# Moving a store to another queue, sums of x to another engine, and read-backs over three chunks

## The chip, the cores and the metric

One core of one Trainium2 chip. The metric is device time in microseconds (us) of the whole kernel, the median of a few runs. The engines named below are TensorE (PE in the profile, PEld its weight loads), VectorE (DVE), ScalarE (ACT), GpSimd (POOL) and SyncE (SP, which here only issues DMAs). Each of ScalarE, GpSimd and SyncE can issue a DMA from its own instruction stream; instructions of one engine run in the order of the program.

## The reference

```python
def hybrid_layer(x, w_in, b_f, lam_p, subln_g, w_out, ln_g, ln_b, layer_idx):   # x (1, 512, 2048) float32
    h = x @ w_in
    (fq, fk, fv, fg, sq, sk, sv, sg, dq, dk, dv, dg, ff) = jnp.split(h, _split_points(), axis=-1)
...
    o_fox = forgetting_attention(...)              # 6 heads of 128
    o_fox = o_fox.reshape(b, s, FOX_W) * jax.nn.silu(fg)
...
    o_sb = stick_breaking_attention(...)           # 6 heads of 128
    o_sb = o_sb.reshape(b, s, SB_W) * jax.nn.silu(sg)
...
    o_d = differential_attention(...)              # 4 heads of 128, then RMS norm of each head
    o_d = of.astype(x.dtype).reshape(b, s, DIFF_W) * jax.nn.silu(dg)

    y = jnp.concatenate([o_fox, o_sb, o_d], axis=-1) @ w_out
    return _layernorm(DEEPNORM_ALPHA * x + y, ln_g, ln_b)
```

All of it is float32. One input projection makes queries, keys, values and gates of 16 heads and the forget gates; three kinds of causal attention follow, each head's output is multiplied by its gate, and one output projection, the residual and a layer norm end it.

## The kernel before

Every float32 operand of a product is split into a rounded part ("h", made by ScalarE as a cast or copy) and the rest ("l", made by VectorE as operand minus rounded part, line 121, 191 or 699), and a product is three matmuls: h times h, h times l, l times h (`mm3`). So each chunk of weights that arrives in a tile `raw` costs one cast on ScalarE and one subtraction on VectorE, and TensorE waits for the "l" part last.

**Stages.** The first stage multiplies x by the weights of the first pair's queries and keys ("f" chunks 0 to 7, 128x2x512 each, accumulators p0a to p0d): every chunk goes through the four accumulators in 36 matmuls. Then come 30 units u = 2 to 31 of four chunks each; a unit is one kind (query, key, value, gate) of one pair of heads, and it uses seven products in the place of eight (a Strassen-like scheme), so that x is needed in sums as well. The last stage is the output projection (accumulators po0a to po3d), which needs the gated outputs of all 16 heads as "m0" to "m15", each split in h and l.

**Sums of x.** x comes in eight tiles `xr` (n = 0 to 7). `split_x` makes the h and l parts used by the first stage; `x_sums` then overwrites the tile with four sums of quarter tiles (lines 331 to 334, 128x256 elements each) and splits the result into `xs_0`, `xs_1` (128x1024 each). The sums are used from unit 2 on. `x_sums(n)` is called at ticks 4n+5 of a counter that advances with the matmuls.

**Finished heads.** `gate(h)` multiplies a head's output `mx` by its gate on GpSimd (line 493) and stores it to a DRAM tensor `mixd` (line 494); the last two heads stay on chip. In the last unit, u = 31, `load_mix` reads the 14 stored heads back on ScalarE's queue (line 505) into tiles `mr` and splits them. Their places become free as x's tiles of that unit are used up, seven to a chunk.

**Order.** The program text is laid out by ticks, and a scheduler that plays a timeline then fixes the order of each engine; matmuls and a few others are pinned in the written order. SyncE fetches the weight chunks (lines 163 and 166) into three `raw` tiles, and GpSimd adds a second part onto each unit chunk by an accumulating DMA (line 172), both far ahead of use.

Of the kernel before, what the change touches and what calls it, by code (L numbers as in the profile page):

```python
# [12 lines left out]
ALU = mybir.AluOpType  # L13
# [6 lines left out]
NK = D // P  # L20
# [58 lines left out]
def trunk(ctx, tc, x, xt, w_first, w_in, w_ff, b_f, lam_p, subln_g, w_out, ln_g, ln_b, out):  # L79
    nc = tc.nc  # L80
    V, A, G, T = nc.vector, nc.scalar, nc.gpsimd, nc.tensor
# [29 lines left out]
    def mm3(ps, ah, al, bh, bl, first, last, part=None):  # L111

        if part in (None, 0):
            mm(ps, ah, bh, first, False)
        if part in (None, 1):
            mm(ps, ah, bl, False, False)
        if part in (None, 2):
            mm(ps, al, bh, False, last)
# [4 lines left out]
    def split(hi, lo, src, scale=None):  # L123

        if scale is None:
            A.copy(hi, src)  # L126
            low(lo, src, hi)
        else:
            A.activation(hi, src, AF.Copy, scale=scale)
            V.scalar_tensor_tensor(out=lo, in0=src, scalar=scale, in1=hi.bitcast(F32),  # L130
                                   op0=ALU.mult, op1=ALU.subtract)
# [7 lines left out]
    NU = 4 * len(PAIRS)  # L139
# [81 lines left out]
    def tick():  # L221
        if clock[0] in events:
            with tc.high_priority(EARLY if clock[0] > T0 else 0):
                for fn in events.pop(clock[0]):
                    fn()
        clock[0] += 1

    def load_ahead(n):
        fetch(n + AHEAD + 2)
        add_in(n + AHEAD + 1)  # L230
        if n + AHEAD < len(chunks) and n + AHEAD not in ready:
            load_chunk(n + AHEAD)
# [28 lines left out]
    def kx_pair(tags, shape, name):  # L261
        return tuple(kx.tile(shape, F32R, tag=t, name=f"{name}{s}") for t, s in zip(tags, "hl"))
# [27 lines left out]
    mixd = dram.tile([NK, P, S], F32, name="mixd")  # L290
# [3 lines left out]
    with ExitStack() as actx:  # L294
# [31 lines left out]
        def x_sums(n):  # L326


            j, i = divmod(n, 2)
            r = xraw.pop(n).rearrange("p k (b t) -> p (k b) t", b=2)  # L330
            G.tensor_tensor(out=r[:, 3], in0=r[:, 1], in1=r[:, 3], op=ALU.subtract)
            G.tensor_tensor(out=r[:, 1], in0=r[:, 1], in1=r[:, 0], op=ALU.subtract)
            G.tensor_tensor(out=r[:, 0], in0=r[:, 3], in1=r[:, 0], op=ALU.subtract)
            G.tensor_tensor(out=r[:, 2], in0=r[:, 2], in1=r[:, 0], op=ALU.add)
            xs[j][i] = kx_pair(xs[j][i], [P, 4, H2], f"xs{j}_{i}")
            split(*xs[j][i], r)

# [136 lines left out]
        def silu(h, c):  # L474

            e = wk(f"ge{h}")
            A.activation(e, c, AF.Abs)
            A.activation(e, e, AF.Exp, scale=-1.0)
            A.activation(e, e, AF.Ln, bias=1.0)
            V.scalar_tensor_tensor(out=e, in0=c, scalar=0.0, in1=e, op0=ALU.min, op1=ALU.subtract)  # L480
            A.activation(e, e, AF.Exp)  # L481
            G.tensor_tensor(out=c, in0=c, in1=e, op=ALU.mult)  # L482
            gt[h] = c
            if h in mixed:
                gate(h)
# [3 lines left out]
        def gate(h):  # L489
            mx = mixed[h]  # L490
            kt = ORDER.index(h)
            if kt < NK - 2:
                G.tensor_tensor(out=mx, in0=mx, in1=gt[h], op=ALU.mult)
                nc.sync.dma_start(mixd[kt], mx)
            else:
                V.tensor_mul(mx, mx, gt[h])
                into_slot(kt, mx)

        def into_slot(kt, src):
            mh[kt], ml[kt] = next_slot(f"m{kt}")  # L500
            split(mh[kt], ml[kt], src)

        def load_mix(kt):
            mr = wk(f"mr{kt}")
            nc.scalar.dma_start(mr, mixd[kt])
            into_slot(kt, mr)
# [119 lines left out]
        def head_out(h, aux):  # L626
            o = o_of[h]
            mx = at.tile([P, S], F32, tag="mx", name=f"mx{h}")
            A.copy(mx, o)
            if not NF + NS <= h:  # L630
                mixed[h] = mx
                if h in gt:
                    gate(h)
                return
            sq = wk(f"sq{h}")
            A.activation(sq, o, AF.Square)
            sqh, sql = wk(f"sqh{h}", F32R), wk(f"sql{h}", F32R)
            split(sqh, sql, sq)
            aux.update(mx=mx, sq=(sqh, sql))

        def sub_norm(h, aux):

            ss = psO(f"ss{h}")
            mm(ss, onesr, aux["sq"][0], True, False)
            mm(ss, onesr, aux["sq"][1], False, True)
            v = wk(f"v{h}")
            V.tensor_scalar(out=v, in0=ss, scalar1=1.0 / HD, scalar2=SUB_EPS, op0=ALU.mult, op1=ALU.add)
            y, t = wk(f"ry{h}"), wk(f"rt{h}")
            rsqrt(v, y, t)
            mx = aux["mx"]  # L650
            V.scalar_tensor_tensor(out=mx, in0=mx, scalar=g8, in1=y, op0=ALU.mult, op1=ALU.mult)
            mixed[h] = mx
            if h in gt:
                gate(h)
# [56 lines left out]
        for n in range(NJ):  # L711
            at_unit(4 * n + 5 - n // 7, lambda n=n: x_sums(n))
# [6 lines left out]
        def bank(u, b):  # L719
            return ps_p.tile([P, 512], F32, tag=f"pj{b}", name=f"p{u}{b}")  # L720
# [77 lines left out]
        for u in range(2, NU):  # L798
            pb = {}
            for j in range(NK // 4):  # L800
                load_ahead(n)
                wp = ready[n]
                xp = {5: 3, 7: 1, 6: 0, 3: 2}
                for m, pr in enumerate(SUMS_LAST if 0 < j < NK // 4 - 1 else BANKWISE):
                    if m % 2 == 0:
                        tick()
                    b, half = BANK[pr]
                    if b not in pb:
                        pb[b] = bank(u, b)
                    dst = pb[b][:, half * H2:(half + 1) * H2]  # L810
                    for i in range(2):
                        if pr == 1:
                            bh, bl = xa[j][0][:, i], xa[j][1][:, i]
                        elif pr in xp:
                            bh, bl = (s[:, xp[pr]] for s in xs[j][i])
                        else:
                            kt, cs = 4 * j + 2 + i, slice(0, H2) if pr == 2 else slice(H2, S)
                            bh, bl = xh[kt][:, cs], xl[kt][:, cs]
                        mm3(dst, wp[pr][0][:, i], wp[pr][1][:, i], bh, bl,
                            j == 0 and i == 0 and half == 0,  # L820
                            j == NK // 4 - 1 and i == 1 and (half == 1 or pr == 3))
                    if j == NK // 4 - 1:
                        with tc.high_priority(EARLY):
                            combine(u, pr, pb)
                del ready[n]
                n += 1
                if u == NU - 1 and j < 2:
                    for kt in range(7 * j, 7 * j + 7):
                        load_mix(kt)

        def out_product(n, k, kt, t, c0, ps):
# [167 lines left out]
```

## Time and profile before

| | |
|---|---|
| median of 3 runs | 1022.93 us (1016.45 to 1025.36) |
| the profiled execution | 1020.78 us, of it 1019.0 us from the first to the last instruction |
| TensorE, VectorE, ScalarE, GpSimd busy | 94%, 74%, 52%, 27% of the span |
| granted TensorE clock, mean | 0.981 |
| DRAM read and written | 151.18 MB and 12.07 MB |

The profile is of one execution. Busy shares are averages over very different stages; a stage is judged by its own window. A time in brackets behind a row of the timeline is how long the engine stood idle before it, and the arrow names what ended that.

### The profile page before, as it was taken

The numbers are of one execution on the slowest core, as the hardware profiler recorded it, in microseconds if no ns is written. First come the engines' busy times: TensorE is split into PE (matmuls) and PEld (weight loads), VectorE is DVE, ScalarE is ACT, GpSimd is POOL, SyncE is SP. The second block draws the span as 40 slices with busy tenths as digits, with TensorE's granted clock in tenths as the row PEclk, the third lists the DMA queues.
The fourth block names the chain that finished last, engine by engine and source line by source line (L and its number), as shares of the span: only waits on it lengthen the run. The fifth ranks groups of instructions, "written<-read, shape, count | busy, mean of one in ns | idle before, by whom it ended". The sixth has DMA issues, their size and how long they took to land.

```text
span 1019.0 us, 18043 instructions
## 1 busy us (share of the span) xinstructions
PE 954.7 (94%) x6944; PEld 899.6 (88%) x6944; DVE 753.0 (74%) x1284; ACT 526.9 (52%) x893; POOL 272.6 (27%) x322
## 2 busy tenths in 40 slices
PE   8798999989998998989999999999999789999994
PEld 7688989989998998979998999999999778888883
DVE  8957787779777976997899778877877853433558
ACT  6445564466455644764576556646754762221222
POOL 6822242224232321231222133223322010000026
PEclk9899999999999999999999999999999999999997
DMA  7365567656665666557656766677677732832313
GB/s 278 110 149 145 136 163 191 166 145 163 176 169 145 157 173 181 130 138 176 176 145 141 191 169 173 168 198 194 168 178 196 231 106 82 349 104 87 108 59 140
DMA packets 53406, 164.42 MB, mean 161 GB/s; under 512 B 6466, under 2 KB 7106, under 8 KB 53064
## 3 DMA queue, kind: packets, MB, share of 16 engines
q1 hardware_dynamic: 29256, 111.36, 33.3%
q0 software_dynamic: 20320, 41.43, 23.6%
q10 hardware_dynamic: 3744, 10.49, 2.8%
q8 instruction: 54, 0.88, 0.4%
q14 instruction: 32, 0.26, 0.1%
HBM read 151.18 MB, written 12.07 MB: 160 GB/s over the span
## 4 chain that ended last, share of the span: by engine, by line
PE 57%; DVE 16%; DMA 14%; issue 6%; ACT 4%; POOL 2%; ACTq 0%; POOLq 0%; DVEq 0%; SPq 0%
PE o L106 9%; DMA raw<-in_w_in_dram 9%; DVE wlt L121 4%; DMA mr<-mixd 2%; PE l L106 2%; DVE wlb L121 2%; ACT wht L126 2%; DMA kc<-qkd 1%; DMA qc<-qkd 1%; PE po0b L106 1%; PE p0a L106 1%; PE po0c L106 1%; PE po0d L106 1%; PE po2d L106 1%; PE po2c L106 1%
## 5 line engine op out<-in xcount | busy, mean ns | idle before, releaser
L172 POOL DMA_DIRECT2D raw<-in_w_in_dram x120 | 104.8, 874 | 447.1 <-DMA raw<-in_w_in_dram 221.9
L121 DVE TENSOR_TENSOR wlt<-raw,wht 128x1024 fp32r<-128x1024 f32 x120 | 151.0, 1263 | 50.5 <-ACT wht L126 49.8
L126 ACT CAST wht<-raw 128x1024 fp32r<-128x1024 f32 x120 | 124.8, 1046 | 104.2 <-DVE raw L204 70.8
L121 DVE TENSOR_TENSOR wlb<-raw,whb 128x768 fp32r<-128x768 f32 x120 | 119.7, 1002 | 25.5 <-ACT whb L126 24.9
L126 ACT CAST whb<-raw 128x768 fp32r<-128x768 f32 x120 | 99.8, 832 | 57.6 <-PE p2d L106 7.8
L203 DVE TENSOR_TENSOR raw<-raw 128x256 f32<-128x256 f32 x120 | 53.5, 448 | 28.3 <-DMA raw<-in_w_in_dram 27.3
L121 DVE TENSOR_TENSOR wl<-raw,wh 128x1024 fp32r<-128x1024 f32 x23 | 30.2, 1314 | 51.4 <-ACT wh L126 51.4
L126 ACT CAST wh<-raw 128x1024 fp32r<-128x1024 f32 x23 | 24.1, 1050 | 63.1 <-PE po2d L106 27.6
L204 DVE TENSOR_TENSOR raw<-raw 128x256 f32<-128x256 f32 x120 | 54.5, 459 | 2.2
L535 ACT ACTIVATE u<-u,m 128x128 f32<-128x128 f32 (+3 forms) x56 | 31.4, 561 | 47.1 <-DVE m L532 46.9
L907 POOL TENSOR_TENSOR y<-y,gb 128x512 f32<-128x512 f32 (+1 forms) x8 | 12.0, 1517 | 155.5 <-ACT y L906 155.5
L126 ACT CAST pth<-pt 128x128 fp32r<-128x128 f32 (+1 forms) x64 | 26.9, 421 | 14.5 <-PE pt L109 14.0
L121 DVE TENSOR_TENSOR ptl<-pt,pth 128x128 fp32r<-128x128 f32 (+1 forms) x64 | 30.9, 483 | 3.5 <-ACT pth L126 3.3
L191 DVE TENSOR_TENSOR wl<-raw,wh 128x512 fp32r<-128x512 f32 x22 | 17.1, 793 | 20.8 <-ACT wh L190 20.8
L571 DVE TENSOR_TENSOR_SCAN rs<-e 128x128 f32<-128x128 f32 (+3 forms) x24 | 19.8, 823 | 15.1 <-POOL e L568 15.1
L482 POOL TENSOR_TENSOR g<-g,ge 128x512 f32<-128x512 f32 x16 | 24.7, 1542 | 16.9 <-ACT ge L481 16.9
L190 ACT CAST wh<-raw 128x512 fp32r<-128x512 f32 x22 | 13.5, 620 | 28.6 <-PE o L106 11.1
L106 PE MATMUL o<-ptl,vh 128*128 128x256 f32 x96 | 27.6, 287 | 0.0
L106 PE MATMUL o<-pth,vl 128*128 128x256 f32 x96 | 27.4, 285 | 0.0
L548 POOL TENSOR_SCALAR_AFFINE_SELECT d<-d 128x128 f32<-128x128 f32 x24 | 16.3, 679 | 39.3 <-ACT d L547 39.3
L106 PE MATMUL o<-pth,vh 128*128 128x256 f32 x96 | 25.6, 267 | 0.0
L576 ACT ACTIVATE rs<-rs 128x128 f32<-128x128 f32 (+3 forms) x24 | 11.3, 470 | 26.8 <-POOL rs L574 26.8
(6285 smaller groups left out, 4010.6 us busy)
## 6 DMA issues: line engine op xcount, KB each, us to landing
raw<-in_w_in_dram SPq DMA_DIRECT2D x120, 640.0 KB, 4.9
raw<-in_w_in_dram POOLq DMA_DIRECT2D x120, 256.0 KB, 4.3
raw<-in_w_out_dram SPq DMA_DIRECT2D x32, 512.0 KB, 3.9
xr<-in_x_t_dram SPq DMA_DIRECT2D x7, 512.0 KB, 7.6
raw<-in_w_first_dram SPq DMA_DIRECT2D x7, 512.0 KB, 5.2
mixd<-mx SPq DMA_DIRECT2D x14, 256.0 KB, 4.1
qkd<-c POOLq DMA_DIRECT2D x14, 256.0 KB, 4.3
mr<-mixd ACTq DMA_DIRECT2D x14, 256.0 KB, 3.6
```

The source lines that it names most:

```text
L106: pin(T.matmul(ps, lhs, rhs, start=start, stop=stop))
L121: V.tensor_tensor(out=lo, in0=src, in1=hi.bitcast(F32), op=ALU.subtract)
L126: A.copy(hi, src)
L172: nc.gpsimd.dma_start(raws[n][:, 0:2], w_in[g - 2, j, :, 1:3], accum_op=ALU.add)
L190: pin(A.copy(hi, raw[:, k]))
L191: pin(V.tensor_tensor(out=lo, in0=raw[:, k], in1=hi.bitcast(F32), op=ALU.subtract))
L203: V.tensor_tensor(out=raw[:, 2], in0=raw[:, 2], in1=raw[:, 0], op=ALU.add)
L204: V.tensor_tensor(out=raw[:, 3], in0=raw[:, 3], in1=raw[:, 2], op=ALU.add)
L482: G.tensor_tensor(out=c, in0=c, in1=e, op=ALU.mult)
L535: A.activation(u[:, :n], u[:, :n], AF.Exp, bias=m, scale=-1.0, accum_out=sm)
L548: G.affine_select(out=dt_[:, i * P:n], in_=dt_[:, i * P:n], pattern=[[-1, P]], base=0, channel_multiplier=1, compare_op=ALU.is_ge, fill=BIG)
L571: V.tensor_tensor_scan(out=rv[:, :n][:, ::-1], data0=ev[:, ::-1], data1=ev[:, ::-1], initial=0.0, op0=ALU.add, op1=ALU.max)
```

## The change

Three edits. The four sums of `x_sums` are issued on VectorE in the place of GpSimd. The store of a gated head is issued on GpSimd's queue in the place of SyncE's. The 14 read-backs are issued as 4, 5 and 5 in the first three chunks of unit 31, in the place of 7 and 7 in the first two.

```diff
             r = xraw.pop(n).rearrange("p k (b t) -> p (k b) t", b=2)
-            G.tensor_tensor(out=r[:, 3], in0=r[:, 1], in1=r[:, 3], op=ALU.subtract)
-            G.tensor_tensor(out=r[:, 1], in0=r[:, 1], in1=r[:, 0], op=ALU.subtract)
-            G.tensor_tensor(out=r[:, 0], in0=r[:, 3], in1=r[:, 0], op=ALU.subtract)
-            G.tensor_tensor(out=r[:, 2], in0=r[:, 2], in1=r[:, 0], op=ALU.add)
+            V.tensor_tensor(out=r[:, 3], in0=r[:, 1], in1=r[:, 3], op=ALU.subtract)
+            V.tensor_tensor(out=r[:, 1], in0=r[:, 1], in1=r[:, 0], op=ALU.subtract)
+            V.tensor_tensor(out=r[:, 0], in0=r[:, 3], in1=r[:, 0], op=ALU.subtract)
+            V.tensor_tensor(out=r[:, 2], in0=r[:, 2], in1=r[:, 0], op=ALU.add)
...
                 G.tensor_tensor(out=mx, in0=mx, in1=gt[h], op=ALU.mult)
-                nc.sync.dma_start(mixd[kt], mx)
+                nc.gpsimd.dma_start(mixd[kt], mx)
...
-                if u == NU - 1 and j < 2:
-                    for kt in range(7 * j, 7 * j + 7):
+                if u == NU - 1 and j < 3:
+                    for kt in range(*((0, 4), (4, 9), (9, NK - 2))[j]):
                         load_mix(kt)
```

TensorE's order is the same to the last matmul. VectorE's list grows by 32 instructions and GpSimd's loses them and gains 14 DMA issues. The scheduler also moves some rows nearby.

The first place is VectorE's list in the first stage, around the "l" part of chunk 3's weights (wl_239, made from raw_174). xr_128, xr_154, xr_168, xr_172, xr_222 and xr_226 are the tiles of x for n = 0 to 5. Before, on VectorE:

```order
L121 TENSOR_TENSOR xb2l<-xr_226,xb2h 128x256
L121 TENSOR_TENSOR x11l<-xr_226,x11h 128x512
L121 TENSOR_TENSOR xs_0l<-xr_168,xs_0h 128x1024
L121 TENSOR_TENSOR wl_239<-raw_174,wh_238 128x1024
L121 TENSOR_TENSOR wl_295<-raw_180,wh_294 128x1024
L121 TENSOR_TENSOR xs_1l<-xr_172,xs_1h 128x1024
```

And now, on the same engine at the same place:

```order
L121 TENSOR_TENSOR xb2l<-xr_226,xb2h 128x256
L121 TENSOR_TENSOR x11l<-xr_226,x11h 128x512
L331 TENSOR_TENSOR xr_172<-xr_172 128x256
L121 TENSOR_TENSOR xs_1l<-xr_154,xs_1h 128x1024
L333 TENSOR_TENSOR xr_168<-xr_168 128x256
L121 TENSOR_TENSOR wl_239<-raw_174,wh_238 128x1024
L331 TENSOR_TENSOR xr_222<-xr_222 128x256
L121 TENSOR_TENSOR wl_295<-raw_180,wh_294 128x1024
```

The sums stand between the other rows, the split of xs_0 from n = 2 has gone behind wl_239, and that of xs_1 from n = 1 has come down to stand just ahead of it.

The second place is GpSimd's list at the first gated head (mx_1459). e_1 and rs_1 are tiles of an attention head's scores, raw_1434 is a weight chunk. Before, on GpSimd (the store stood on SyncE, between two weight fetches):

```order
L482 TENSOR_TENSOR g_1320<-g_1320,ge_1394 128x512
L493 TENSOR_TENSOR mx_1459<-mx_1459,g_1320 128x512
L568 AFFINE_SELECT e_1_1479<-e_1_1479 128x128
L172 DMA raw_1434<-in_w_in_dram 128x512
L574 AFFINE_SELECT rs_1_1485<-rs_1_1485 128x128
```

And now:

```order
L482 TENSOR_TENSOR g_1320<-g_1320,ge_1394 128x512
L493 TENSOR_TENSOR mx_1459<-mx_1459,g_1320 128x512
L568 AFFINE_SELECT e_1_1479<-e_1_1479 128x128
L494 DMA mixd<-mx_1459 128x512
L172 DMA raw_1434<-in_w_in_dram 128x512
L574 AFFINE_SELECT rs_1_1485<-rs_1_1485 128x128
```

The store follows its own product on the engine that made it, and the accumulating fetch comes behind it.

The third place is ScalarE's list at the end of unit 31. wh_1 is the rounded half of the output projection's first chunk, without which TensorE can't go on in po0a; wh_10147 and wh_10232 belong to the two chunks after it, m10h and m12h are read-backs. Before, on ScalarE:

```order
L126 CAST pth_2_10018<-pt_3_10151 128x4x128
L535 ACTIVATE u_0_10119,s_0_10122<-u_0_10119,m_0_10120 128x128
L765 COPY e_10170<-p31a 128x2x256
L553 ACTIVATE u_0_10119<-u_0_10119,r_0_10124 128x128
L126 CAST wh_10232<-raw_10074 128x1024
L535 ACTIVATE u_1_10211,s_1_10214<-u_1_10211,m_1_10212 128x256
L190 CAST wh_1_10080<-raw_9822 128x512
```

And now:

```order
L505 DMA mr_10141<-mixd 128x512
L126 CAST m10h<-mr_10125 128x512
L126 CAST wh_10147<-raw_9919 128x1024
L126 CAST m10h<-mr_10131 128x512
L126 CAST pth_2_10004<-pt_3_10151 128x4x128
L547 ACTIVATE d_1_10202<-cb_10082,ncq 128x256
L553 ACTIVATE u_0_10093<-u_0_10093,r_0_10098 128x128
L126 CAST m12h<-mr_10135 128x512
L765 COPY e_10170<-p31a 128x2x256
L126 CAST m12h<-mr_10141 128x512
L126 CAST wh_10232<-raw_10048 128x1024
L190 CAST wh_1_10054<-raw_9822 128x512
```

Casts of read-backs, which had all been done before this piece, now stand in it, ahead of wh_1.

## Rows read from the trace of the kernel before

**Rows 1.** The page: busy time by engine, and the chain that ended last.

```profile
PE 954.7 (94%) x6944; PEld 899.6 (88%) x6944; DVE 753.0 (74%) x1284; ACT 526.9 (52%) x893; POOL 272.6 (27%) x322
...
PE 57%; DVE 16%; DMA 14%; issue 6%; ACT 4%; POOL 2%; ACTq 0%; POOLq 0%; DVEq 0%; SPq 0%
```

**Rows 2.** Windows of the first stage: busy time of each engine, clock, DMA.

```profile
8.20:31.30 23.10, 15.72 (x92) 13.11 (x90) 23.10 (x24) 16.48 (x30) 20.25 (x19) 0.93 0.61 221
31.30:52.00 20.70, 20.66 (x122) 18.80 (x123) 20.65 (x17) 6.94 (x7) 17.23 (x15) 0.91 0.46 130
```

**Rows 3.** Timeline of TensorE: start, length, instruction, and idle time before it.

```profile
31.34 0.58 PE L106 MATMUL p0a<-xa1h,wl 128*128 128x256 f32 x1 [6.87 <-DVE wl L121]
```

**Rows 4.** The chain that ended last, first stage: start, length, what.

```profile
12.38 1.44 PE p0a L106 x7
...
18.04 1.73 PE p0a L106 x9
...
38.63 1.41 PE p0a L106 x9
...
59.73 1.41 PE p0d L106 x9
```

**Rows 5.** Timeline of VectorE in the first stage.

```profile
6.33 0.42 DVE L121 TENSOR_TENSOR xb0l<-xr,xb0h 128x256 fp32r<-128x256 f32 x1
6.66 0.42 DVE L698 CAST wh<-raw 128x512 fp32r<-128x512 f32 x1
7.00 0.68 DVE L121 TENSOR_TENSOR x2l<-xr,x2h 128x512 fp32r<-128x512 f32 x1
7.60 0.68 DVE L699 TENSOR_TENSOR wl<-raw,wh 128x512 fp32r<-128x512 f32 x1
...
13.13 0.96 DVE L121 TENSOR_TENSOR xb1l<-xr,xb1h 128x256 fp32r<-128x256 f32 x1
14.01 1.23 DVE L121 TENSOR_TENSOR x6l<-xr,x6h 128x512 fp32r<-128x512 f32 x1
...
29.54 3.41 DVE L121 TENSOR_TENSOR wl<-raw,wh 128x1024 fp32r<-128x1024 f32 x2
...
57.09 0.76 DVE L204 TENSOR_TENSOR raw<-raw 128x256 f32<-128x256 f32 x2
58.76 1.23 DVE L121 TENSOR_TENSOR wlt<-raw,wht 128x1024 fp32r<-128x1024 f32 x1 [0.92 <-ACT wht L126]
59.91 0.69 DVE L130 SCALAR_TENSOR_TENSOR ql<-qr,qh 128x512 fp32r<-128x512 f32 x1
```

**Rows 6.** Timeline around the first store, SyncE and VectorE.

```profile
134.18 0.33 SPq L494 DMA_DIRECT2D mixd<-mx  x1
...
135.69 1.22 DVE L121 TENSOR_TENSOR wlt<-raw,wht 128x1024 fp32r<-128x1024 f32 x1
...
136.93 0.33 SPq L163 DMA_DIRECT2D raw<-in_w_in_dram  x1
```

**Rows 7.** Line 454, GpSimd's own stores: ns of one, min/median/max.

```profile
L454 POOL DMA_DIRECT2D qkd<-c x14: 576/606/902, 146.7 to 768.7; - x14
```

**Rows 8.** Timeline of TensorE, unit 31 and the start of the output projection.

```profile
804.20 0.38 PE L106 MATMUL p31a<-xs_0h,wht 128*128 128x256 f32 x1 [2.75 <-ACT wht L126]
...
806.19 0.44 PE L106 MATMUL p31a<-xs_0h,wlt 128*128 128x256 f32 x1 [1.49 <-DVE wlt L121]
...
811.96 0.66 PE L109 MATMUL pt<-ident,u 128*128 128x128 f32 x4 [1.03 <-ACT u L553]
...
820.77 0.50 PE L106 MATMUL po0a<-wh,m1h 128*128 128x512 f32 x1 [1.23 <-ACT wh L190]
...
822.72 0.50 PE L106 MATMUL po0a<-wl,m1h 128*128 128x512 f32 x1 [1.45 <-DVE wl L191]
```

**Rows 9.** Timeline of ScalarE there, and the page's row of the read-backs (KB, us to landing).

```profile
810.66 0.62 ACT L126 CAST m10h<-mr 128x512 fp32r<-128x512 f32 x1 [2.53 <-DMA mr<-mixd]
...
820.12 0.60 ACT L190 CAST wh<-raw 128x512 fp32r<-128x512 f32 x1
...
mr<-mixd ACTq DMA_DIRECT2D x14, 256.0 KB, 3.6
```

## The prediction

> **What bounds the kernel now.** The busy table comes first: TensorE is busy for 94% of the span, and it holds 57% of the chain that ended last [rows 1]. So a gain can only come from a place where TensorE waits, and each of the three edits has to be tied to such a place. The windows of the first stage show one: from 8.2 to 31.3 us VectorE is busy all the time, 23.1 of 23.1 us, GpSimd 20.25 of them with the sums of x, and TensorE only 15.72; in the next 20.7 us VectorE still has no gap, and the granted clock is 0.91 of full [rows 2]. The timeline gives the wait its name: at 31.34 TensorE takes up chunk 3 after 6.87 us, released by VectorE's subtraction for that chunk's "l" part [rows 3]. The chain shows what it cost after that: in chunk 1 the third matmul starts at 12.38 and the next chunk's row at 18.04, 5.66 us; in chunk 3 it is 31.34 to 38.63, 7.29 us, 1.63 more, because the clock had fallen to its lower level (1.2 GHz) in the pause [rows 4]. Chunks 4 to 7 then run without a wait and the stage ends at 59.73 + 1.41 = 61.14 [rows 4]. The stage thus loses 6.87 + 1.63 = 8.5 us at one place, and VectorE is late there. The other place is the end of unit 31: waits of 2.75, 1.49, 1.03, 1.23 and 1.45 us within 19 us, released by ScalarE and VectorE, which have the read-backs in their lists [rows 8].
>
> **Sums of x on VectorE.** VectorE is saturated there, and it gets 32 more instructions. What decides is that its own instructions were slow while GpSimd summed. Without GpSimd, starts follow each other by 0.34 us for 128x256 (6.33, 6.66, 7.00) and 0.60 for 128x512 (7.00, 7.60), and 1.15 for 128x1024 (58.76, 59.91); beside GpSimd's sums the same 128x256 takes 0.88 (13.13, 14.01), a 128x512 lasts 1.23 instead of 0.68, and two 128x1024 last 3.41 together, about 1.7 each [rows 5]. The DMA engines are no likely cause: their share falls from 0.61 to 0.46 between the two windows of rows 2, and GpSimd's load stays.
>
> The sum up to chunk 3's "l" part goes by the orders. Before, 22 instructions stand from 8.20 to its end at about 31.25: 10 of 128x256, 7 of 128x512, 5 of 128x1024. By the fast prices they are 10 x 0.34 + 7 x 0.60 + 5 x 1.15 = 13.35 us, so some 9.7 of the 23 us are interference. Now 33 instructions stand there: one 128x1024 (the split of xs_0 from n = 2) has gone behind, and 12 sums have come ahead. That is 13.35 - 1.15 + 12 x 0.34 = 16.3, and the part is ready at 24.5 instead of 31.25. TensorE would ask for it at about 23.6 (chunks 1 and 2 gain about 0.8 from the same source), so a wait of 1 us is left and VectorE is still last, and I take it that the clock, which fell after 6.87 us, stays up after so short a pause. Gain: 31.3 - 24.5 = 6.8 of start and 1.6 of clock, **8.4 us**.
>
> Is something late next? Up to the first "l" part of stage two (from 58.76 to 59.99 before [rows 5], for TensorE's 61.14) VectorE's list now has 32 sums, 14 lows of 128x256, 11 of 128x512, 14 of 128x1024 and some 5 us of smaller work: 10.9 + 4.8 + 6.6 + 16.1 + 4.8 = 43.2 us from 8.20, so 51.4. TensorE wants it at 61.14 - 8.4 = 52.7. It fits with 1.3 us to spare; before, the margin was 1.15. The price of a sum isn't in the trace; its bounds are 0.34 and 0.88 by the rows, and I take 0.34, since L204, a sum of the same shape and in place, made two in 0.76 us at 57.09 with GpSimd idle [rows 5].
>
> The Trainium skill, SBUF — State Buffer, section on who interferes with whom, has a rule that bears on this: a VectorE instruction with two SBUF inputs and a GpSimd instruction that reads SBUF share one port as an exclusive lock, and the second to issue waits for the whole of the first. The rows agree that two-input instructions stretch, but by 0.54 us at 128x256, less than a whole sum of GpSimd; by either reading the sums alone on VectorE meet no lock, and the term stays.
>
> **Stores on GpSimd's queue.** On SyncE the store waits for GpSimd's product with the next weight fetch behind it. At the first store the fetch goes out at 136.93, 2.4 us after the store's issue ended, and just when VectorE's subtraction, which frees the `raw` tile, ends at 135.69 + 1.22 = 136.91 [rows 6]. I read the 13 other stores in the same way, and at each the next fetch leaves at the end of such a subtraction. So SyncE's relief is worth **nothing**. On GpSimd a store costs its issue, 0.58 to 0.90 us by its own stores of the same size, median 0.61 [rows 7]: 14 x 0.61 = 8.5 us of an engine that is busy for 27% [rows 1]. Queued behind it are the accumulating fetches and the masks of scores; GpSimd mostly waits for a landing or for VectorE ahead of these, which covers the issue. Ends: 0 and 14 x 0.90 = 12.6 us; I take 0. SyncE loses 14 issues, and no queue is passed by anything else.
>
> **Read-backs as 4, 5, 5.** Nothing is taken away; ten of the 28 splits come later. What gains is chunk 2's "t" part on ScalarE and VectorE: with two fewer read-backs ahead of it, 1 to 2 us of the 2.75 + 1.49 [rows 8]. What loses is wh_1: before, it stood at 820.12 with all read-backs done [rows 9]; now the casts of the last five stand ahead of it, and they are issued only at about 810 and need 3.6 us to land, during which ScalarE stands still as it did for 2.53 us at 810.66 [rows 9]. From there: landing at 814, then five casts of 0.52, two of weights of 1.0, the other softmax rows and the copy of p31a of about 2.4, and wh_1 at 820 to 821 again. So TensorE comes earlier to po0a and waits longer in it. Bounds: all waits of rows 8 gone, 8 us, and one more landing exposed, -3.6; I take **0.5 us** of gain, as the same casts are on ScalarE either way.
>
> **Sum.** 8.4 + 0 + 0.5 = 9 us. Against the profiled execution, 1020.8 - 9 = 1011.8; the median of the runs lies 2.1 higher, so 1022.9 - 9 = **1014 us**. The reordering near it, in the units of the second and third pair, moves rows by one or two places where TensorE doesn't wait; I give it 0 with 1.5 us each way.
>
> **Rivals.** Times are on the scale of the median.
>
> 1. The read-back really opens the end: half of the waits in rows 8 go, 4 us in the place of 0.5, 1010. For it: chunk 2 is freed of two splits. Against: wh_1 is now last in ScalarE's list. 17%.
> 2. The read-back closes it: one more landing of 3.6 is exposed ahead of wh_1, 1014 + 4 = 1018. For it: ScalarE's new order. 16%.
> 3. The first stage's gain is only half carried on: a late x tile or a late first chunk of stage two takes its place; 1014 + 4.3 = 1018. For it: the margin of 1.3 us. Against: every fetch that feeds it is triggered by VectorE's own earlier subtractions. 9%.
> 4. The stores hold GpSimd on the path: up to 12.6 us, 1014 + 12.6 = 1027, at half exposure 1020. For it: DMA is 14% of the chain [rows 1], and the accumulating fetches are issued behind the stores. Against: GpSimd's idle time. 6%. Here the skill speaks against the change: the same page says that a DMA issued from GpSimd can starve under VectorE's work and took 3.1 us in the place of 0.62, and by that figure 14 stores would be an estimated 43 us of GpSimd. The stores of rows 7 ran beside a VectorE that is 74% busy, and none took over 0.90.
> 5. Slower than before: the stretch was not GpSimd's doing, and VectorE gets 32 sums on top. The first "l" part of stage two then comes at 60 + 32 x 0.34 = 71 or, at the slow price, 60 + 28 = 88 instead of 61: 1033 to 1050. It decides from the point where a sum costs more than about 0.6 us with its neighbours unchanged. Against it are the fast and slow rows of the same shape. 4%.
>
> **How the numbers follow.** The forecast itself has 48%, as 1009 to 1018. The range 1007 to 1021 takes in rivals 1 to 3 and half of 4. About 1% is what a measurement of this kernel can tell from no change, that is 1012.7 and below for faster: rival 1 and a third of the forecast, with a little for noise, 0.36; slower is rival 5 and a part of 4, 0.07; the rest, 0.57, is within.
>
> **What would show it.** In the profile after: two-input instructions of VectorE at 0.34, 0.60 and 1.15 us steps from 8 to 50 us; the wait of 6.87 gone to about 1 and the clock at full there; the first stage ending near 52.7; no PE wait behind a store on GpSimd; the waits at the start of po0a longer than before and those of chunk 2 shorter. I am wrong if VectorE's steps stay at 0.88, if the stage ends early but unit 2 starts late, or if the end moves by more than 4 us.

## The result, and the profile after

The changed kernel takes 1008.43 us in the median (four runs, 1007.21 to 1010.7) against 1022.62 for the kernel before: ratio 0.9872, 95% interval 0.9824 to 0.9920, so 8 to 18 us faster. The measured median lies inside the range given (1007 to 1021), 5.6 us under the forecast of 1014 and 0.6 under the stretch of 1009 to 1018 that the forecast itself was given; it is nearest to rival 1. The profiled execution took 1007.21 us, span 1005.5, 13.5 less than before.

The start of a unit's first matmul is the best ruler through the span, since TensorE's order is the same in both:

```
start of        before    after   difference
p2 (stage two)   60.98    52.36     -8.62
p7              189.00   180.84     -8.16
p14             365.79   363.46     -2.33
p24             626.15   615.13    -11.02
p31             785.81   774.46    -11.35
po2             916.59   902.10    -14.49
```

So the first stage brings 8.6 us, the 29 units after it 2.7 net (they lose 6 and win 9), unit 31 with the start of the output projection 3.1, and 1.0 is lost behind po2, which makes 13.5.

The page's busy table, to compare with [rows 1] (the chain of the profile after goes back only to 789 us, so its shares can't be compared):

```profile
PE 954.1 (95%) x6944; PEld 903.0 (90%) x6944; DVE 744.4 (74%) x1316; ACT 528.7 (53%) x893; POOL 246.1 (24%) x304
```

VectorE has 32 instructions more and 8.6 us less busy time: what it lost was stretch. The windows of the first stage, as [rows 2] (length, then busy time of PE, PEld, DVE, ACT and POOL, clock, DMA share, GB/s):

```profile
8.20:24.50 16.30, 15.50 (x97) 13.77 (x96) 16.30 (x34) 13.04 (x25) 0.00 (x0) 1.00 0.77 284
8.20:31.30 23.10, 22.30 (x140) 19.91 (x139) 23.10 (x49) 16.82 (x30) 0.00 (x0) 1.00 0.80 292
31.30:52.00 20.70, 20.70 (x135) 18.84 (x134) 19.02 (x34) 11.00 (x14) 3.32 (x4) 1.00 0.49 111
```

VectorE does 49 instructions in the 23.1 us in which it did 24, and the granted clock is 1.00. VectorE's timeline, as [rows 5], and TensorE's wait, as [rows 3]:

```profile
12.51 0.42 DVE L121 TENSOR_TENSOR xa1l<-xr,xa1h 128x256 fp32r<-128x256 f32 x1
12.84 0.42 DVE L121 TENSOR_TENSOR xb1l<-xr,xb1h 128x256 fp32r<-128x256 f32 x1
13.18 0.69 DVE L121 TENSOR_TENSOR x6l<-xr,x6h 128x512 fp32r<-128x512 f32 x1
13.78 0.42 DVE L333 TENSOR_TENSOR xr<-xr 128x256 f32<-128x256 f32 x1
...
23.09 1.22 DVE L121 TENSOR_TENSOR wl<-raw,wh 128x1024 fp32r<-128x1024 f32 x1
...
51.31 1.23 DVE L121 TENSOR_TENSOR wlt<-raw,wht 128x1024 fp32r<-128x1024 f32 x1 [0.66 <-ACT wht L126]
...
24.36 0.38 PE L106 MATMUL p0a<-xa1h,wl 128*128 128x256 f32 x1 [0.80 <-DVE wl L121]
```

Steps are 0.34 us at 128x256 where they were 0.88, and 0.60 at 128x512. Chunk 3's "l" part ends at 24.31 (forecast 24.5), TensorE waits 0.80 us for it instead of 6.87, and VectorE comes to stage two's first "t" part at 51.31 after a gap of 0.66, so its list is no longer what is late. The part ends at 52.54; TensorE, which starts the stage at 52.36, takes it up at 53.30 and doesn't wait.

The stores: GpSimd's timeline at the first one, and line 494's own view (ns of one, min/median/max). The store's issue took 0.61 us, landings take 2.3 to 3.9 us:

```profile
125.13 0.47 POOL L568 TENSOR_SCALAR_AFFINE_SELECT e<-e 128x128 f32<-128x128 f32 x1
125.56 0.61 POOL L494 DMA_DIRECT2D mixd<-mx  x1
127.04 0.86 POOL L172 DMA_DIRECT2D raw<-in_w_in_dram  x1 [0.87 <-DMA raw<-in_w_in_dram]
...
L494 POOL DMA_DIRECT2D mixd<-mx x14: 597/613/613, 125.6 to 753.4; - x14
...
DMA to landing us min/median/max: 2.3/2.9/3.9
```

Behind the store GpSimd stood idle for 0.87 us until a landing, so the store was covered. TensorE's waits in unit 31 and at the output projection, as [rows 8], and ScalarE there, as [rows 9]:

```profile
790.86 0.39 PE L106 MATMUL p31a<-xs_0h,wht 128*128 128x256 f32 x1 [1.25 <-ACT wht L126]
793.09 0.58 PE L106 MATMUL p31a<-xs_0h,wlt 128*128 128x256 f32 x1 [1.72 <-DVE wlt L121]
806.37 0.50 PE L106 MATMUL po0a<-wh,m1h 128*128 128x512 f32 x1 [0.85 <-ACT wh L190]
808.31 0.50 PE L106 MATMUL po0a<-wl,m1h 128*128 128x512 f32 x1 [1.44 <-DVE wl L191]
...
789.76 1.05 ACT L126 CAST wht<-raw 128x1024 fp32r<-128x1024 f32 x1
...
798.46 0.62 ACT L126 CAST m9h<-mr 128x512 fp32r<-128x512 f32 x1 [0.26 <-DMA mr<-mixd]
...
804.23 0.62 ACT L126 CAST m12h<-mr 128x512 fp32r<-128x512 f32 x1 [0.84 <-DMA mr<-mixd]
804.75 1.04 ACT L126 CAST wh<-raw 128x1024 fp32r<-128x1024 f32 x1
805.70 0.61 ACT L190 CAST wh<-raw 128x512 fp32r<-128x512 f32 x1
```

The waits add up to 5.26 us instead of 7.95 (2.75 + 1.49 + 1.03 + 1.23 + 1.45), and the one for the softmax row is gone in this execution. ScalarE's last stop for a landing is 0.84 us instead of the 2.53 at 810.66. wh_1 stands at 805.70, 31.2 us after the start of unit 31; before it was 820.12 - 785.81 = 34.3.

The middle was not in the forecast. VectorE, GpSimd and TensorE at the change from unit 8 to unit 9 (c is the combination of unit 8; TensorE needs its bank b for p9b):

```profile
231.65 1.23 DVE L121 TENSOR_TENSOR wlt<-raw,wht 128x1024 fp32r<-128x1024 f32 x1 [0.38 <-ACT wht L126]
232.79 0.95 DVE L571 TENSOR_TENSOR_SCAN rs<-e 128x384 f32<-128x384 f32 x1
233.66 1.46 DVE L766 TENSOR_TENSOR e<-e 128x256 f32<-128x256 f32 x1
...
236.43 0.95 DVE L121 TENSOR_TENSOR wlb<-raw,whb 128x768 fp32r<-128x768 f32 x1
237.30 0.41 DVE L778 TENSOR_TENSOR c<-p8b,e 128x256 f32<-128x256 f32 x1
...
232.99 1.84 POOL L482 TENSOR_TENSOR g<-g,ge 128x512 f32<-128x512 f32 x1
...
237.86 0.36 PE L106 MATMUL p9b<-xs_0h,wht 128*128 128x256 f32 x1 [2.56 <-DVE c L778]
```

And before:

```profile
239.12 1.16 DVE L766 TENSOR_TENSOR e<-e 128x256 f32<-128x256 f32 x1
...
241.13 1.21 DVE L121 TENSOR_TENSOR wlt<-raw,wht 128x1024 fp32r<-128x1024 f32 x1
242.51 0.96 DVE L571 TENSOR_TENSOR_SCAN rs<-e 128x384 f32<-128x384 f32 x1 [0.17 <-POOL e L568]
243.38 0.40 DVE L778 TENSOR_TENSOR c<-p8b,e 128x256 f32<-128x256 f32 x1
...
243.93 0.36 PE L106 MATMUL p9b<-xs_0h,wht 128*128 128x256 f32 x1
```

The weight row wlt and the score row rs, which stood behind the combination's first step (L766), now stand ahead of it, and wlb and another score row (L573) have come in ahead of its step for bank b (L778). So L766 starts 0.66 us after TensorE has begun p9a (233.66 and 233.00) where it started 2.08 ahead (239.12 and 241.20). A gate product of GpSimd stretches it to 1.46 us, but it took 1.16 before as well. Unit 13 has the same wait, 2.55 us. Before, neither p9b nor p13b waited for the combination.

The waits are the smaller part of what the middle loses. These are the windows from p7 to p14, before and after (columns as above):

```profile
189.00:365.79 176.79, 165.86 (x1347) 161.86 (x1346) 144.63 (x227) 101.21 (x167) 54.47 (x72) 1.00 0.65 163
180.84:363.46 182.62, 169.78 (x1347) 167.54 (x1346) 146.04 (x227) 102.18 (x167) 59.04 (x75) 0.96 0.64 159
```

Of the 5.8 us lost, TensorE's idle time makes 1.9 (10.93 to 12.84), and the same 1347 matmuls took 3.9 us longer at a lower granted clock: it is 0.50, the level of 1.2 GHz, behind both waits, from 239.4 to 242.7 and from 341.8 to 345.1. From p14 to p24 the gain of 8.7 is 5.3 us less idle time (15.20 to 9.88) and 3.4 us of faster matmuls, at 0.99 instead of 0.97.

### The profile page after: what moved, and what is told of

It is laid out like the page before. It is cut to its first block, busy times and chain, and to the rows that moved or that the text cites. A ratio compares the mean times of both kernels' runs of the same rounds, so it can differ in the third digit from the quotient of the medians.

```text
span 1005.5 us, 18030 instructions
## 1 busy us (share of the span) xinstructions
PE 954.1 (95%) x6944; PEld 903.0 (90%) x6944; DVE 744.4 (74%) x1316; ACT 528.7 (53%) x893; POOL 246.1 (24%) x304
## 5 line engine op out<-in xcount | busy, mean ns | idle before, releaser
L121 DVE TENSOR_TENSOR wlt<-raw,wht 128x1024 fp32r<-128x1024 f32 x120 | 147.9, 1237 | 48.4 <-ACT wht L126 48.0
L121 DVE TENSOR_TENSOR wlb<-raw,whb 128x768 fp32r<-128x768 f32 x120 | 121.5, 1015 | 28.7 <-ACT whb L126 27.8
L121 DVE TENSOR_TENSOR wl<-raw,wh 128x1024 fp32r<-128x1024 f32 x23 | 28.1, 1222 | 50.9 <-ACT wh L126 50.9
L191 DVE TENSOR_TENSOR wl<-raw,wh 128x512 fp32r<-128x512 f32 x22 | 14.8, 689 | 21.1 <-ACT wh L190 21.1
L574 POOL TENSOR_SCALAR_AFFINE_SELECT rs<-rs 128x128 f32<-128x128 f32 x24 | 19.3, 804 | 27.1 <-DVE rs L573 26.2
```

What stands on the lines that cost most here:

```text
L121: V.tensor_tensor(out=lo, in0=src, in1=hi.bitcast(F32), op=ALU.subtract)
L191: pin(V.tensor_tensor(out=lo, in0=raw[:, k], in1=hi.bitcast(F32), op=ALU.subtract))
L574: G.affine_select(out=rv[:, i * P:n], in_=rv[:, i * P:n], pattern=[[-1, P]], base=-1, channel_multiplier=1, compare_op=ALU.is_ge, fill=-BIG)
```

## The experiments

Twelve runs, in three groups, each group timed against the kernel before on its own chip (its median there: 1023.08, 1020.92 and 1018.82), with ten executions each and four of `sums_spread`, `gates_v` and `both`. Ratios are to the kernel before; they are estimated from all executions and need not be quotients of the medians (for `store` that quotient is 1.0008).

**Each edit alone, and the change without the store.** The edits are those of the diff above: `sums` has only the four sums on VectorE, `store` only the store, `spread` only the 4, 5, 5; `sums_spread` leaves the store on SyncE.

> Only the sums of x go to VectorE; stores and read-backs stay as before. Theory (GpSimd's sums stretched VectorE's steps, so the 'l' parts of the first chunks came late): VectorE's steps in the first stage at 0.34, 0.60 and 1.14 us again, unit 2 starts near 52.4 us in the place of 60.98, and the median is 8 to 9 us under the kernel before, near 1014. The stretch from unit 31 to po2 stays at 130.8 us, as before. Rival (the start's gain needs the store's move or is partly paid back as VectorE gets fuller): unit 2 starts at 52.4, but the median is 1017 to 1019.

> Only the store of a finished head goes to GpSimd's queue. Theory (SyncE was never late, GpSimd has time for an issue of 0.9 us): the median is the same within 2 us, near 1022; unit 2 starts at 61.0 and the stretch from unit 31 to po2 stays at 130.8 us. Rival A (SyncE's stores held weight fetches up, and the 2.4 us that the middle units won come from here): units 3 to 30 are 2 us or more shorter than before, median near 1020. Rival B (an issue holds GpSimd and the work behind it): up to 12 us longer, near 1034.

> Only the read-backs go 4, 5, 5 in three chunks. The changed kernel was 3.1 to 3.5 us shorter from unit 31 to po2. Theory (all of this is the spread's: ScalarE reaches the output projection's first cast sooner): unit 31 to po2 in 127.6 us in the place of 130.8, median near 1019.5, unit 2 at 61.0 as before. Rival (the spread is worth the 0.5 us of the forecast, and the end gained because the store's move or an earlier fetch opened it): 130.3 us, median near 1022.

> All of the change but the store's move. Theory (the store's move is worth nothing): the median is within 2 us of the changed kernel's 1008.4, start and end as there (unit 2 at 52.4, unit 31 to po2 in 127.6 us). Rival A (the store's move won the middle's 2.4 us): 1011. Rival B (the store's move disturbs the order of rows and costs the 6 us that units 9 to 14 lost): 1004 or less, with no such loss there.

```
             median    ratio [95%]                p2      p31 to po2
sums         1014.14   0.9929 [0.9894, 0.9963]   52.35    131.50
store        1023.93   0.9976 [0.9935, 1.0016]   61.55    132.88
spread       1019.90   0.9971 [0.9944, 0.9997]   61.27    131.49
sums_spread  1010.85   0.9878 [0.9833, 0.9924]   52.35    123.68
```

The sums alone bring the whole start. The store alone can't be told from nothing; its stretch from unit 31 to po2 was 2.1 us longer than the 130.8 expected. The spread alone is faster by 0.3 us to 5.7 us, about 3 in the middle of the interval; but its profiled execution, at 1027.41 the slowest of its ten, shows no gain in unit 31, so its place isn't shown by that trace. The three ratios multiplied give 0.988, the change's 0.987: the edits add up, within intervals of 3 to 5 us each way. Without the store the median is 1010.85, which is rival A's number and just outside the theory's 2 us; but on that chip the ratio is 0.9878, the whole change's was 0.9872, so no worth of the store's move shows, within the 5 us of these intervals.

**Idle work on GpSimd.** The changed kernel with 32 instructions put back on GpSimd, on a scratch tile, in three kinds: the loops stand in `x_sums`, the first in `dum2`, the second in `dum1`, the third, with memsets twice as many, in `dum0`. Line numbers in these kernels are 2 to 4 higher.

```diff
+        spare_t = at.tile([P, S], F32, tag="kx", name="spare_t")
+        G.memset(spare_t, 0.0)
...
+            for _ in range(4):
+                G.tensor_tensor(out=spare_t[:, H2:], in0=spare_t[:, :H2], in1=spare_t[:, H2:], op=ALU.add)
...
+            for _ in range(4):
+                G.tensor_copy(spare_t[:, H2:], spare_t[:, :H2])
...
+            for _ in range(8):
+                G.memset(spare_t, 0.0)
```

> The changed kernel, with 32 idle sums put back on GpSimd (two inputs, 128x256, on a scratch tile that nothing else uses), run back to back from the start to about 30 us. Theory (a GpSimd instruction with inputs in SBUF shares something with VectorE's two-input instructions, whoever's data it is): VectorE's steps stretch again (0.34 to 0.88 us at 128x256), unit 2 starts 5 to 9 us later than in the changed kernel (57 to 61 in the place of 52.4), median 1014 to 1018. Rival (the steps were long in the kernel before because VectorE waited for, or shared tiles with, those sums): unit 2 at 52.4, median near 1008.

> As the one before, but the 32 idle instructions on GpSimd are copies (one input, 128x256). Theory: still an input read from SBUF, so VectorE is stretched as by the sums, as long as a copy runs; unit 2 at 55 to 60. Rival (only GpSimd instructions of two inputs stretch it): unit 2 at 52.4, median near 1008.

> As the one before, but the 32 idle instructions are 64 memsets of 128x512 (no input at all), about as long in sum. Theory (it is GpSimd's reading that VectorE waits for): nothing is stretched, unit 2 at 52.4, median near 1008. Rival (any GpSimd access to SBUF stretches VectorE, writes too): unit 2 at 55 or later.

Medians 1026.23, 1012.84 and 1012.81; ratios 1.0043 [1.0007, 1.0079], 0.9933 [0.9896, 0.9970] and 0.9890 [0.9854, 0.9926]; unit 2 starts at 69.60, 56.12 and 52.77. With two inputs, a window and VectorE's timeline of `dum2`, and one of the idle sums while VectorE had nothing to do:

```profile
8.20:24.50 16.30, 10.42 (x49) 8.93 (x50) 16.30 (x17) 8.16 (x17) 15.04 (x17) 0.79 0.57 215
...
11.18 0.96 DVE L333 TENSOR_TENSOR xr<-xr 128x256 f32<-128x256 f32 x1
12.06 0.96 DVE L121 TENSOR_TENSOR xa0l<-xr,xa0h 128x256 fp32r<-128x256 f32 x1
12.94 0.94 DVE L121 TENSOR_TENSOR xb0l<-xr,xb0h 128x256 fp32r<-128x256 f32 x1
...
2.58 0.73 POOL L338 TENSOR_TENSOR spare_t<-spare_t 128x256 f32<-128x256 f32 x1
```

With one input, `dum1`: the copies on GpSimd end at 1.76 + 15.32 = 17.08, and VectorE's steps change there from 0.54 to 0.34 (below them, one copy while VectorE stood idle):

```profile
1.76 15.32 POOL L338 COPY spare_t<-spare_t 128x256 f32<-128x256 f32 x26
...
15.67 0.61 DVE L121 TENSOR_TENSOR xa1l<-xr,xa1h 128x256 fp32r<-128x256 f32 x1
16.20 0.61 DVE L121 TENSOR_TENSOR xb1l<-xr,xb1h 128x256 fp32r<-128x256 f32 x1
16.74 0.88 DVE L121 TENSOR_TENSOR x6l<-xr,x6h 128x512 fp32r<-128x512 f32 x1
...
20.55 0.41 DVE L336 TENSOR_TENSOR xr<-xr 128x256 f32<-128x256 f32 x1
20.89 0.41 DVE L121 TENSOR_TENSOR xa1l<-xr,xa1h 128x256 fp32r<-128x256 f32 x1
...
2.22 0.40 POOL L338 COPY spare_t<-spare_t 128x256 f32<-128x256 f32 x1
```

With none, `dum0`: GpSimd is as busy and VectorE is untouched:

```profile
8.20:24.50 16.30, 15.41 (x94) 13.47 (x92) 16.30 (x34) 12.71 (x24) 14.69 (x29) 1.00 0.76 280
...
12.93 0.41 DVE L121 TENSOR_TENSOR xa1l<-xr,xa1h 128x256 fp32r<-128x256 f32 x1
13.26 0.41 DVE L121 TENSOR_TENSOR xb1l<-xr,xb1h 128x256 fp32r<-128x256 f32 x1
```

The scratch tile is nobody else's, so it is not data but the reading that VectorE waits for: 0.54 us for a two-input instruction of 128x256, 0.20 for a copy, nothing for a memset. In `dum2` the two engines alternate, 17 and 17 instructions in 16.3 us, and the cost is the sum. Four of the 32 sums ran before VectorE had work, so 28 x 0.54 = 15.1 us; VectorE's list is 14.94 us later than in the changed kernel from then on (xb2l's first at 34.01 instead of 19.07). Unit 2 starts 69.60 - 52.36 = 17.24 later; the other 2.3 us are TensorE's, which waited 6.19 us for chunk 3's "l" part up to 39.29 and then had a granted clock of 0.50 until 44.4. In `dum1` 7 of the 26 copies ran before VectorE had work, and 19 x 0.20 = 3.8, for 56.12 - 52.36 = 3.76. For `dum2` I had expected 57 to 61 and 1014 to 1018, by the kernel before; there VectorE didn't have the 32 sums itself. `dum0`'s median is above the 1008 expected, but its ratio is the changed kernel's (0.9872 and, below, 0.9896).

**The change without the spread**, `sums_store`.

> The change without the spread of the read-backs. Theory (edits add up: the sums about 9 us, the spread about 3, the store none): 1012 to 1015, unit 2 at 52.4; units 9 and 13 wait 2.5 us for the combination of the unit before (line 778), as in both kernels with the store moved. Rival (the spread is worth nothing, the store's move gives the rest): 1008 to 1010.

1011.81, ratio 0.9914 [0.9883, 0.9945], unit 31 to po2 in 132.12 us. The median lies just under the theory's 1012 to 1015 and above the rival's 1008 to 1010. Units 9 and 13 wait again, 3.47 and 2.63 us.

**A second profile, and three versions.** `after_again` is the changed kernel unchanged. `gates_v` moves the gate products, `spread4` spreads the read-backs further, `both` does both:

```diff
-            G.tensor_tensor(out=c, in0=c, in1=e, op=ALU.mult)
+            V.tensor_tensor(out=c, in0=c, in1=e, op=ALU.mult)
...
-                G.tensor_tensor(out=mx, in0=mx, in1=gt[h], op=ALU.mult)
+                V.tensor_tensor(out=mx, in0=mx, in1=gt[h], op=ALU.mult)
...
-                if u == NU - 1 and j < 3:
-                    for kt in range(*((0, 4), (4, 9), (9, NK - 2))[j]):
+                if u == NU - 1:
+                    for kt in range(*((0, 3), (3, 6), (6, 10), (10, NK - 2))[j]):
```

> The changed kernel a second time, unchanged, for a second profile. Theory (the middle's loss in units 8 to 14 and its return up to unit 24 belong to the order of the rows): the starts of units lie within 1.5 us of the first profile, the 2.5 us waits of units 9 and 13 are there again, median 1007 to 1010. Rival (the middle differs from execution to execution): the starts of units differ by 3 us or more after unit 7, and so do its runs, 1005 to 1015.

> The changed kernel with the two products of the gates (lines 482 and 493, 30 of 128x512 on GpSimd at 1.5 us) on VectorE as well. Theory (each two-input product on GpSimd of 128x256 costs VectorE 0.54 us, so one of 128x512 about 1.1 us, an estimate, against 0.60 us to do it itself; units 9 and 13 wait for the stretched combination): the waits of units 9 and 13 fall under 1.5 us, median 1002 to 1006. Rival (in the middle VectorE has slack, so nothing comes back, and a product that waits for its gate holds VectorE's list): 1010 to 1016.

> The changed kernel with the read-backs 3, 3, 4, 4 in all four chunks of unit 31. Theory (ScalarE's casts of what is read back push back the casts that TensorE waits for, so fewer of them in a chunk are better): unit 31 to po2 in 125 to 127 us in the place of 127.6, median 1006 to 1008. Rival (the last four come too late for the output projection): waits for m10 to m13 in po0, 130 us or more, median 1010 or more.

> The two before this together. Theory: both gains add, 1000 to 1005. Rival: no better than the better of the two.

```
             median    ratio [95%]               p7-p15  p15-p24  p28-po2  p31-po2
before                                            201.89  235.26   198.93   130.78
after                                             204.68  229.61   195.46   127.64
after_again  1007.36   0.9896 [0.9861, 0.9931]   203.71  225.82   195.47   127.65
gates_v      1003.44   0.9859 [0.9808, 0.9910]   197.42  232.62   195.56   127.74
spread4      1010.00   0.9926 [0.9888, 0.9963]   204.56  231.41   197.95   127.38
both         1004.71   0.9875 [0.9824, 0.9927]   197.06  231.39   198.71   130.89
```

The second profile repeats the first to 1.6 us up to unit 20, and the waits of p9b and p13b (2.07 and 2.66); from unit 21 on it runs ahead, 3.8 us by unit 24. So the loss in units 8 to 14 belongs to the order, and a part of the regain to the execution: the truth lies between theory and rival. The end repeats to 0.01 us, but only in sum: from p31 to po0 it is 30.2 us in the first profile and 33.0 in the second, from po0 to po2 97.4 and 94.7, and the softmax row that TensorE no longer waited for in the first costs 3.43 us in the second. That agreement is chance.

`gates_v` beats both kernels in the median, 4 us under the changed one on the same chip, though the two intervals overlap. VectorE and TensorE at unit 9:

```profile
230.83 0.51 DVE L766 TENSOR_TENSOR e<-e 128x256 f32<-128x256 f32 x1 [0.19 <-ACT e L765]
...
235.25 0.41 DVE L778 TENSOR_TENSOR c<-p8b,e 128x256 f32<-128x256 f32 x1
...
236.65 0.28 PE L106 MATMUL p9b<-xs_0h,wht 128*128 128x256 f32 x1
```

The first step takes 0.51 instead of 1.46 us (1.16 in the kernel before), the combination is done 1 us before TensorE wants it, and units 7 to 14 are 7.3 us shorter; 3.0 of it go back up to unit 24. The scheduler also moved rows there, so stretch and order aren't separated by this run. `spread4` gains nothing on 4, 5, 5: unit 31 to po2 stays within 0.3 us, and 2.8 are lost in units 28 to 30, ahead of it. The rival's median came (1010.00) without its cause: the waits for m10 to m13 didn't come, but po0a waits 2.93 us for VectorE's "l" part of its weights. `both` lies inside the theory's 1000 to 1005 but is no better than `gates_v`, as the rival has it; its po0a waits 3.42 us.

## Why the prediction was right, and where not

- **Sums of x: right, by its own steps.** Forecast 8.4, measured 8.62 in the first profile and 8.5 to 8.8 in every kernel with the sums on VectorE and nothing added. The part was ready at 24.31 (24.5), the remaining wait 0.80 (1), the clock full, stage two at 52.36 (52.7). The price of a sum was the lower bound, 0.34. The margin at stage two was mis-stated: the 43.2 us had no idle time in them, VectorE stood 1.7 us for ScalarE's casts, and the part ended at 52.54, not 51.4; it cost nothing because TensorE takes it up 0.94 us after the stage's first matmul. The idle instructions show the cause, which the forecast had only argued: GpSimd's reads. The Trainium skill, SBUF — State Buffer, section on who interferes with whom, has the same cases, reads against two-input VectorE instructions and no contention with a GpSimd instruction that only writes, and `dum0` agrees (no change). Its lock for the "whole instruction", which stands in the page's section on the two sides of SBUF, is more than the rows show: VectorE lost 0.54 us to a sum that takes 0.73 alone (`dum2`) and 0.20 to a copy that takes 0.40 alone (`dum1`), so the measurement decides. Rivals 3 and 5 fell.
- **Stores: right.** 0 forecast; alone 0.9976 with no change inside the interval, and 0.9878 against 0.9872 left out, each within about 5 us. Issues took 0.60 to 0.61 us beside a VectorE that is 74% busy; rival 4's 3.1 us were not seen.
- **Read-backs: the direction was right, the term too small.** 0.5 forecast; the runs say about 3: 0.9971 alone (0.3 to 5.7 us), 0.9914 without it against 0.9872 and 0.9896 with it, and from unit 31 to po2 130.8 to 132.9 us in the four profiles with 7 and 7 against 123.7 to 129.4 in seven with 4, 5, 5 (131.5 for the spread alone). That is rival 1. The term for chunk 2 was right in the first profile, 4.24 us of waits become 2.97, where 1 to 2 was forecast; the waits in po0a, forecast longer, are 2.29 us instead of 2.68. The step that failed is "and wh_1 at 820 to 821 again". On that scale it came at 817.0 (785.81 + 31.2). I had the last five issued at about 810; four of them went out at 806.0 to 807.8 and the last at 809.8. And I had let ScalarE stand still for a whole landing of 3.6 us before the last five casts, in the place of the 2.53 that it stood before; it stood for 0.26 and 0.84, because between those issues and landings it now has the cast of wh_10147 and the copy of p31a to do, which came after all read-backs before. Eleven of the twelve profiles with either spread agree: with 7 and 7 ScalarE waits 6.4 to 8.8 us for landings of read-backs in unit 31 (four profiles) and wh_1 stands 34.3 to 36.5 us behind the unit's start; with 4, 5, 5 (eight profiles) it waits 2.7 to 5.0, and wh_1 stands at 28.8 to 33.1, but for the spread alone, at 34.2. The lower bound thus had the sign wrong: here, spreading the transfers hides landings.
- **The reordering: wrong where it says that TensorE doesn't wait there; its net is open.** "0 with 1.5 us each way" for units 2 to 30; the two profiles have 2.7 and 6.6 us of gain, beyond the bounds, but that it is the change's isn't shown: the same stretch, 724.8 us before, took 722.1 and 718.2 in the changed kernel's two profiles and 714.9 to 732.0 in the eleven others, and 8.6 + 3 us for the other two terms lie within the intervals of the ratios. In all eight profiles with the store on GpSimd's queue and the gate products still there, p9b and p13b wait 2.1 to 3.5 us for the combination; in none of the four with the store on SyncE. Those four have in its place a wait of 1.25 to 2.03 us in p15a for ScalarE's copy of unit 14 (line 765), which the others lack. The waits part the two groups; the lengths don't: units 7 to 14 took 203.7 to 211.2 us in the eight and 201.9 to 205.8 in the four, units 15 to 23 225.8 to 234.8 and 230.7 to 235.8. So rows that the scheduler put elsewhere, for an edit with no measurable worth itself, move waits of 1 to 3.5 us from one place to another, and the time also goes by the clock behind them, which the forecast left out here. I looked at where TensorE waited before, and not at the combination, where it would wait if VectorE's rows came in another order.

The forecast of 9 us was thus 8.4 + 0 + 0.5 where the profiled execution has 8.6 + 3.1 + 2.7 - 1.0 = 13.4, the 1.0 lost behind po2. The total stayed in the range because its largest term was right; the read-backs' term was too small and, in these profiles, so was the reordering's, to the same side.

What stays open: why executions of one kernel differ by 5 us and more from unit 21 on (the changed kernel 1003.27 to 1015.27 in ten runs), which single profiles can't show; and what the regain up to unit 24 owes to the change: p15a's 2.03 us are part of 5.3 us less idle time, and 3.4 are the clock's.

## What to carry to other kernels

If VectorE is late in a stage and GpSimd reads SBUF beside it, price GpSimd's instruction by what it takes from VectorE: here 0.54 us for a sum that VectorE does itself in 0.34. Count it both ways before handing work to GpSimd. A change of one queue can move rows far from it: look for the results that TensorE needs soonest after them (here the combination that frees a bank), not only for the places where it waits already, and count the clock behind a new wait (here 1.9 us more idle time and 3.9 us of slower matmuls). When transfers are spread, ask what the waiting engine does in the meantime before charging a landing to it.

## What the runs showed of the hardware

The stretch of a VectorE instruction beside GpSimd is a fixed time per instruction, whatever the VectorE instruction's size: +0.54 us at 128x256, 128x512 (11.18 to 12.06, and 14.67 to 15.80 for 0.60) and 128x1024 (17.53 to 19.19 for 1.13), and +0.20 beside copies. A GpSimd product of 128x512 took about 1 us (L766, 1.46 for 0.41), about twice that of 128x256. The stretch is less than the GpSimd instruction takes alone: 0.54 of 0.73 us for a sum, 0.20 of 0.40 for a copy. A cast on VectorE of 128x512, one input, was stretched by the same amount (8.01 to 8.88 in `dum2` instead of 0.34). And the same store landed in 2.9 us from GpSimd's queue, 4.1 from SyncE's before; in `gates_v`, also from GpSimd's queue, it took 4.9, so the queue alone isn't shown to be the cause.
